# First FFN of a hybrid encoder trunk: second product by Strassen's algorithm, in a written order of three engines

## The chip, the core and the metric

The kernel runs on one core of one Trainium2 chip. The metric is device time in microseconds for one launch, from inputs in HBM to the output in HBM; the median of several runs is given. TensorE (PE) does the matrix products, VectorE (DVE) and ScalarE (ACT) the elementwise work, SyncE (SP) issues nearly all DMA transfers.

## The reference

One sequence of 512 tokens, model width 1024, two layers. Each layer is a token mixer (a short gated convolution in layer 0, a Mamba-2 SSD mixer in layer 1) followed by a SwiGLU FFN of width 2816. Each of these four sub-layers normalises, scales and shifts its input, and gates its normalised output by vectors that are computed from the conditioning vector c ("adaLN"):

```python
mod = (jax.nn.silu(c) @ ada_w + ada_b).reshape(bsz, DEPTH, 2, 3, D_MODEL)
...
shift, scale, gate = (mod[:, i, 1, k][:, None, :] for k in range(3))
h = rmsnorm(x, norm_g[i, 2]) * (1.0 + scale) + shift
gate, up = jnp.split(h @ w_in, 2, axis=-1)          # in swiglu_ffn
y = (jax.nn.silu(gate) * up) @ w_out                # 512x2816 @ 2816x1024
x = x + gate * rmsnorm(y, norm_g[i, 3])
```

All data are float32.

## The kernel before

Every float32 product is done in three matmuls: each operand is split into a rounded high part (a cast by ACT) and the low remainder (a subtraction by DVE), and high x high, high x low and low x high are summed in PSUM (`mm3`, `mm_tiles`, `product`). So each weight that arrives by DMA costs one ACT cast and one DVE subtraction (`split_w`) before TensorE can use it.

The first product of an FFN (`in_chunk`) makes one 128-feature block for all 512 tokens in 24 matmuls of 512 columns: 8 blocks of the inner dimension, three matmuls each. Features are taken in pairs, two gate blocks and two up blocks, so four chunks a pair and 11 pairs. In the first FFN (`ffn`), `ff_act` takes SiLU (ACT), multiplies by up (DVE) and splits the result for the second product.

The second product (`out_begin`) sums 22 feature blocks into four token tiles by two column halves, three matmuls each. Its end is interleaved with the next stage's beginning by `Boundary`: squares and roots for the norm, the residual `x`, the next norm `xn`, its transposes `tr`, scale and shift `u`, the split `hi`/`lo`, and the first matmuls `k` of the next stage for six feature blocks whose weights were made ahead (`lead`). The order of PE, ACT and DVE there is the written list `BOUNDARY`. Tokens 0 to 255 go first, tokens 256 to 511 after; `rest` finishes the second half's matmuls.

adaLN's product runs on DVE: `ada_madd` multiplies 512 columns of one 128-row block of `ada_w` by a column of c and adds it up; 8 of them are a set (2 MB of `ada_w`, loaded by `ada_load` in four transfers). `ada_keep` transposes and reduces the set, and `ada_fin` ends a unit of two sets with a small matmul and a few short DVE operations. There are 20 sets. In the first FFN `ada_next` does fourteen of them, interleaved with the feature pairs, and `put_gates` sends the gates through DRAM.

Outside blocks under `manual_schedule` a planner places the instructions: in the first FFN all engines, in the boundaries only those not named there. SP's order is the planner's everywhere but in the opening. Each engine and SP's queue run strictly in their order.

The last FFN (`last_ffn`) already does its second product by Strassen's algorithm. Activations are split into a 2 x 2 of blocks (two feature blocks of a pair, two token halves), weights into a 2 x 2 (two feature blocks, two column halves). `ff_pair` writes the activations and their sums, `build_sums` adds up the weight blocks and stores them in DRAM (`td`). Pass one multiplies three of the seven terms for all pairs, pass two the other four; `pa`, `pb`, `pz` are PSUM accumulators.

Of the kernel before, what the change touches and what calls it, by code (L numbers as in the profile page):

```python
# [35 lines left out]
def trunk_kernel(  # L36
# [52 lines left out]
    def turned(rws, cls, n):  # L89
        pt = aux_ps("ptr")  # L90
        pe.transpose(pt[:, :n], rws[:n, :], ident[:n, :n])
        dve.tensor_copy(cls, pt[:, :n])

    def other_vectors(stage):
# [9 lines left out]
        turned(stage[:, 0, :], mng, 16)  # L104
        turned(stage[:, 1, :], mcb, 32)
        turned(stage[:, 2, :], cols3, P)
        turned(d_rows.rearrange("p a b -> p (a b)"), dcol, 16)
# [182 lines left out]
    def w_at(w, hl, kk):  # L290
        return w[kk // 4][:, hl, kk % 4, :] if isinstance(w, list) else w[:, hl, kk, :]
# [90 lines left out]
    def out_begin(s, w, get_act, K, gg, xn_tile, first, lead, after):  # L382
# [47 lines left out]
        class Boundary:  # L430
# [21 lines left out]

            def sq(self, hf, t):
                st = self.st[t]
                if hf == 0:
                    st["s2"] = small(2)
                act.activation(self.junk(t, hf), ys[hf][t], AF.Square, accum_out=st["s2"][:, hf:hf + 1])

            def yg_(self, hf, t):
                self.yg[hf, t] = t2("yg")  # L460
                dve.tensor_mul(self.yg[hf, t], ys[hf][t], gg[0][:, self.cols(hf)])

            def b1(self, _, t):
                st = self.st[t]
                st["b1"] = small(1)
                dve.tensor_scalar(st["b1"], st["s2"][:, 0:1], 1.0 / D, EPS, MUL, ADD)

            def rt1(self, _, t):
                st = self.st[t]
                st["s1"] = small(1)  # L470
                act.activation(st["s1"], st["s2"][:, 1:2], AF.Sqrt, bias=st["b1"], scale=1.0 / D)
# [80 lines left out]
            def run(self, step):  # L552
                name, i = step.split("_")
# [3 lines left out]
                do(n, int(i))  # L557

# [47 lines left out]
    with ExitStack() as ph:  # L606
        ada_p.append(ph.enter_context(tc.tile_pool(name="adap", bufs=3, reuse_waits="tile")))
        actp = ph.enter_context(tc.tile_pool(name="actp", bufs=22, reuse_waits="tile"))
        gx = ph.enter_context(tc.tile_pool(name="gx", bufs=1, reuse_waits="tile"))
# [294 lines left out]
        def ffn_after(i):  # L904
            return lambda: load_w([(f_w_in[i], DFF + 256, 256)])

        begun = out_finish(out_begin(0, w_out0, lambda k: acts[k], KD, [gg], xn_tile, "aux",
                                     ffn_lead(0, tile4), ffn_after(0)))


        def ffn(s, i, begun, act_tile, gg_tile, xn_tile, ada, gates, lead, after):
            w1, w2 = f_w_in[i], f_w_out[i]
            acts = []
            h, lead_ps, rest, more = begun

            def ff_act(psg, psu, f):
                g = t2("g")
                act.activation(g, psg, AF.Silu)
                dve.tensor_mul(g, psu, g)
                a = act_tile(f"ff{f}")  # L920
                act.copy(a[:, 0, :], g)
                dve.tensor_tensor(a[:, 1, :], g, a[:, 0, :].bitcast(F32), SUB)
                acts.append(a)

            for f in range(0, NF, 2):
                if f == 0:
                    with tc.manual_schedule(engines={PE_ENGINE}):
                        for i in (0, 2, 1, 3, 4, 5):
                            rest(i)
                    pss = lead_ps[:4]  # L930
                elif f == 2:
                    pss = lead_ps[4:] + [in_chunk(w, h) for w in more]
                else:
                    pss = [in_chunk(w, h) for w in load_w([(w1, f * P, 256)]) + load_w([(w1, DFF + f * P, 256)])]
                for b in range(2):
                    ff_act(pss[b], pss[2 + b], f + b)
                ada(f)
                if f == 4:
                    list(vectors)
                if f == 18:  # L940
                    for q in gates:
                        put_gates(q)
                    gg = make_gg(s, gg_tile)
# [739 lines left out]
```

## Time and profile before

| | us |
|---|---|
| median of 3 runs (lowest, highest) | 1350.49 (1350.07, 1351.97) |
| the profiled execution | 1349.98 |
| its span, first to last instruction | 1348.1 |
| PE busy / DVE busy / ACT busy | 1337.3 / 912.0 / 561.7 |
| DMA moved, mean rate | 224.22 MB, 166 GB/s |

The stages of the first FFN, read off the order of matmuls in time: boundary from the convolution to about 222 us, first product to about 460, second product and boundary to the SSD layer from there to about 595. The last FFN runs from about 980 to the end.

In the rows quoted below, a group row gives line, engine, operation, output<-inputs, shape and count, then busy time in us and mean ns of one instruction, then the engine's idle time before them and what ended it. A row of waits gives who waited for whom: total us, times, longest us. A row of a stretch A:B gives for each engine its busy us and, in brackets, its instructions, then TensorE's granted clock, the mean busy share of the DMA engines, and GB/s. A timeline row begins with start and duration in us.

### The profile page before, as it was taken

What the parts mean: (1) busy time and instruction counts of PE and PEld (TensorE: products, weight loads), DVE (VectorE), ACT (ScalarE), POOL (GpSimd) and SP (SyncE); (2) the same over time, 40 slices, a digit from 0 to 9 for tenths busy, and PEclk for the clock granted to TensorE, in tenths of its full rate; (3) what the DMA queues carried; (4) which work ended last, traced back from release to release, by engine and by line L of the source; (5) the groups of instructions that cost most, each with busy time, mean ns of one, the idle gap of its engine ahead of it and who ended that gap; (6) DMA issues with size and microseconds to landing.
All of it is one profiled execution on the core that took longest, in us unless ns stands there. A gap on an engine that the chain in (4) does not pass through costs nothing.

```text
span 1348.1 us, 17657 instructions
## 1 busy us (share of the span) xinstructions
PE 1337.3 (99%) x6957; PEld 1124.6 (83%) x6957; DVE 912.0 (68%) x1512; ACT 561.7 (42%) x866; POOL 10.7 (1%) x27
## 2 busy tenths in 40 slices
PE   8999999999999999999999999999999999999997
PEld 7788889888888888898888888888899888888886
DVE  5799756787864222669888887787575555335884
ACT  5432346222222212655554445564473222223781
POOL 0000000000000000000000000000000000000000
PEclk9999999999999999999999999999999999999999
DMA  9978661577753222414543334423425987223752
GB/s 311 301 239 263 214 208 61 183 240 266 258 194 110 94 95 93 129 33 144 165 149 110 113 107 134 132 71 110 159 68 180 331 285 278 97 71 135 250 193 79
DMA packets 164759, 224.22 MB, mean 166 GB/s; under 512 B 7444, under 2 KB 112580, under 8 KB 162244
## 3 DMA queue, kind: packets, MB, share of 16 engines
q1 hardware_dynamic: 159776, 208.20, 47.3%
q10 hardware_dynamic: 4004, 12.77, 3.0%
q0 software_dynamic: 896, 2.11, 0.5%
q8 instruction: 55, 0.90, 0.3%
q14 instruction: 28, 0.23, 0.1%
HBM read 209.26 MB, written 13.80 MB: 165 GB/s over the span
## 4 chain that ended last, share of the span: by engine, by line
PE 97%; SPq 2%; DMA 1%; DVE 0%; issue 0%; ACT 0%; DVEq 0%; ACTq 0%
PE ip L294 19%; PE ip L295 18%; PE ip L296 18%; PE y L395 6%; PE y L397 6%; PE y L396 6%; PE li L294 3%; PE li L296 3%; PE li L295 3%; PE li L778 2%; PE yd L1185 1%; PE pb L1557 1%; PE pb L1559 1%; PE pb L1558 1%; SPq L641 1%; PE yo L1178 1%
## 5 line engine op out<-in xcount | busy, mean ns | idle before, releaser
L294 PE MATMUL ip<-h,whl 128*128 128x512 f32 x1096 | 431.2, 393 | 0.0
L296 PE MATMUL ip<-h,whl 128*128 128x512 f32 x1096 | 426.9, 389 | 0.0
L295 PE MATMUL ip<-h,whl 128*128 128x512 f32 x1096 | 426.6, 389 | 0.0
L294 PEld LDWEIGHTS ip<-h,whl 128*128 128x128 f32 x1096 | 205.8, 188 | 44.2 <-issue 2.4
L296 PEld LDWEIGHTS ip<-h,whl 128*128 128x128 f32 x1096 | 205.7, 188 | 43.4
L295 PEld LDWEIGHTS ip<-h,whl 128*128 128x128 f32 x1096 | 205.8, 188 | 41.5
L225 ACT CAST whl<-wst 128x1024 fp32r<-128x1024 f32 (+1 forms) x127 | 114.9, 926 | 190.2 <-PE ip L296 159.6
L226 DVE TENSOR_TENSOR whl<-wst,whl 128x1024 fp32r<-128x1024 f32 (+1 forms) x127 | 133.4, 1069 | 71.1 <-ACT whl L225 71.0
L146 DVE SCALAR_TENSOR_TENSOR ada_acc<-ada_st,csil,ada_acc 128x512 f32<-128x512 f32 x140 | 104.5, 748 | 24.2 <-DMA ada_st<-in_ada_w_dram 21.9
L226 DVE TENSOR_TENSOR whlo<-wsto,whlo 128x1024 fp32r<-128x1024 f32 x46 | 56.3, 1223 | 93.2 <-ACT whlo L225 93.1
L225 ACT CAST whlo<-wsto 128x1024 fp32r<-128x1024 f32 x46 | 48.3, 1051 | 111.1 <-PE y L397 83.6
L294 PE MATMUL li<-h,whl 128*128 128x256 f32 x288 | 83.3, 289 | 0.0
L296 PE MATMUL li<-h,whl 128*128 128x256 f32 x288 | 81.5, 283 | 0.0
L295 PE MATMUL li<-h,whl 128*128 128x256 f32 x288 | 81.5, 283 | 0.0
L395 PE MATMUL y<-whlo,ff 128*128 128x512 f32 x176 | 68.6, 390 | 0.0
L397 PE MATMUL y<-whlo,ff 128*128 128x512 f32 x176 | 68.5, 389 | 0.0
L396 PE MATMUL y<-whlo,ff 128*128 128x512 f32 x176 | 68.5, 389 | 0.0
L1052 DVE SCALAR_TENSOR_TENSOR cu<-ip,cols,cu 128x511 f32<-128x511 f32 (+2 forms) x84 | 62.7, 746 | 2.0
L244 DVE TENSOR_TENSOR whl<-wst,whl 128x1024 fp32r<-128x1024 f32 x46 | 55.0, 1218 | 8.0 <-ACT whl L243 7.9
L295 PEld LDWEIGHTS li<-h,whl 128*128 128x128 f32 x288 | 55.3, 192 | 0.0
L294 PEld LDWEIGHTS li<-h,whl 128*128 128x128 f32 x288 | 55.2, 192 | 0.0
L296 PEld LDWEIGHTS li<-h,whl 128*128 128x128 f32 x288 | 55.2, 192 | 0.0
(291 smaller groups left out, 1964.8 us busy)
## 6 DMA issues: line engine op xcount, KB each, us to landing
ada_st<-in_ada_w_dram SPq DMA_DIRECT2D x96, 512.0 KB, 5.6
wst<-in_f_w_in_dram SPq DMA_DIRECT2D x43, 1024.0 KB, 5.7
wst<-in_m_w_in_dram SPq DMA_DIRECT2D x14, 1024.0 KB, 5.3
tb<-in_f_w_out_dram SPq DMA_DIRECT2D x22, 512.0 KB, 7.2
td<-tb SPq DMA_DIRECT2D x11, 1024.0 KB, 7.7
wsto<-in_f_w_out_dram SPq DMA_DIRECT2D x10, 1024.0 KB, 4.9
wst<-in_m_w_in_dram SPq DMA_DIRECT2D x20, 512.0 KB, 4.1
wst<-in_a_w_in_dram SPq DMA_DIRECT2D x9, 1024.0 KB, 5.2
```

What stands on the lines that cost most here:

```text
L146: dve.scalar_tensor_tensor(acc, w, csil[:, k:k + 1], acc, MUL, ADD)
L225: act.copy(dst[:, 0, :nk, :], src)
L226: dve.tensor_tensor(dst[:, 1, :nk, :], src, dst[:, 0, :nk, :].bitcast(F32), SUB)
L244: lambda sw=sw, w=w: dve.tensor_tensor(w[:, 1, :nk, :], sw, w[:, 0, :nk, :].bitcast(F32), SUB)))
L294: pe.matmul(dst, w_at(w, 0, kk), a[:, 0, sl], start=start, stop=False)
L295: pe.matmul(dst, w_at(w, 0, kk), a[:, 1, sl], start=False, stop=False)
L296: pe.matmul(dst, w_at(w, 1, kk), a[:, 0, sl], start=False, stop=stop)
L395: pe.matmul(pst, a[:, 0, tk], wt[:, 0, kk, :], start=k == 0, stop=False)
L396: pe.matmul(pst, a[:, 0, tk], wt[:, 1, kk, :], start=False, stop=False)
L397: pe.matmul(pst, a[:, 1, tk], wt[:, 0, kk, :], start=False, stop=k == K - 1)
L778: pe.matmul(acc_of(i), w[:, part // 2, k, c0:c0 + P], h[kk][:, part % 2, :], start=(kk, part) == (0, 0), stop=(kk, part) == (KD - 1, 2))
L1052: dve.scalar_tensor_tensor(u[:, sft:], pst[:, :T - sft], w[3 - sft], u[:, sft:], MUL, ADD)
```

## The change

- The first FFN's second product becomes Strassen's, in two passes over eleven block pairs, like the last FFN's. The weight sums are made during the first product and go through DRAM (`td`, tensors te0 to te10).
- From the end of the previous boundary to the start of the SSD layer, PE, ACT and DVE run in the program's written order. `Queue` hands out adaLN steps (two multiply-adds each) and weight sums between the chunks: five steps and one set of sums per pair.
- The last four steps of the product are kept for a new boundary list, in which the four quadrants come out one after the other: `c12`, `d`, `c22`, `c21` are the recombinations on DVE, `ma`, `pb`, `p4` the products on PE.
- The weights for the SSD layer's first six chunks are made during the product (`load_ssd`, `make_ssd`).
- adaLN: one set moves to the convolution's boundary, eleven stay in the first FFN, two move to the last FFN, with the gate that they make. Four small vector transposes move to the convolution's boundary and use the other PSUM banks. The first layer's activation pool is closed before the FFN and the new pool takes its place in memory.

```diff
+    STRASSEN_BOUNDARY = """
+ma0 ma1 sq0_0 c12_0 yg0_0 sq1_0 b1_0 yg1_0 rt1_0 rc1_0 x0_0 x1_0 xs0_0 xs1_0 b3_0 rt3_0 pb_0 sq0_1
+c12_1 yg0_1 sq1_1 b1_1 yg1_1 rt1_1 rc3_0 rc1_1 xn0_0 xn1_0 p4_0 x0_1 x1_1 xs0_1 d_0 xs1_1 b3_1
+c22_0 rt3_1 pb_1 c21_0 sq1_2 rc3_1 yg0_2 sq0_2 xn1_1 xn0_1 b1_2 yg1_2 rt1_2 tr0_0 d_1 tr0_1 u0_0
+rc1_2 p4_1 c22_1 u0_1 x0_2 hi0_0 hi0_1 lo0_0 sq1_3 lo0_1 u0_2 xs0_2 u0_3 tr0_2 hi0_2 k0_0 c21_1
+hi0_3 lo0_2 sq0_3 lo0_3 b1_3 yg0_3 u0_4 tr0_3 u0_5 yg1_3 k0_1 hi0_4 x1_2 hi0_5 rt1_3 lo0_4 xs1_2
+lo0_5 k0_2 rc1_3 u0_6 x0_3 hi0_6 x1_3 xs0_3 k0_3 lo0_6 b3_2 xs1_3 rt3_2 b3_3 rc3_2 u0_7 rt3_3
+xn0_2 xn1_2 rc3_3 hi0_7 xn1_3 xn0_3 k0_4 lo0_7 tr1_0 tr1_1 u1_0 k0_5 u1_1 hi1_0 hi1_1 lo1_0 lo1_1
...
+        next(conv_parts[0])
+        list(vectors)
+        ada_next(1)
+        begun = out_finish(conv_parts)
+        ph0.close()
...
-                for b in range(2):
-                    ff_act(pss[b], pss[2 + b], f + b)
-                ada(f)
...
+        def first_ffn(begun, pool):
...
+            def sums_of(g):
...
+                dve.tensor_tensor(b11, b11, b12, ADD)
+                dve.tensor_tensor(b12, b12, b22, ADD)
+                dve.tensor_tensor(b22, b22, b11, ADD)
+                dve.tensor_tensor(b21, b21, b22, ADD)
+                dma(td[g], st)
+                yield
+            def ada_steps():
...
+                for n, (c0, kh) in enumerate(todo):
+                    if kh == 2 and n > 3 and c0 % D == 0:
+                        ada_fin(*ada_open.pop(0))
...
+                    for k in range(2):
+                        ada_madd(acc, st[n][:, k, :], kh * 2 + k)
+                    if n + 3 < len(todo):
+                        st.append(ada_load(*todo[n + 3]))
+                    if kh == 3:
+                        ada_keep(c0, acc)
+                    yield
...
+                def add(self):
+                    next(self.sums.pop(0))
+                    self.load_sums()
...
+            with tc.manual_schedule(engines={PE_ENGINE, mybir.EngineType.Activation, mybir.EngineType.DVE}):
...
+                for g in range(2, NG2):
...
+                    pss = [in_chunk(now[0], h)]
...
+                        load_pair(2 * g + 2)
+                    gs = [silu(pss[0])]
+                    split(0)
+                    jobs.step()
+                    pss.append(in_chunk(now[1], h))
...
+                    gs.append(silu(pss[1]))
+                    split(1)
+                    jobs.add()
+                    jobs.step()
+                    pss.append(in_chunk(now[2], h))
...
+                    up0(pss[2], gs[0])
+                    split(2)
+                    jobs.step(2)
...
+                    pss.append(in_chunk(now[3], h))
...
+                    up1(pss[3], gs[1])
+                    split(3)
+                    jobs.step()
...
+                for i in range(N2 - TAIL):
+                    a6, a22, w8, w4 = ready[i][:4]
+                    if i < NG2:
+                        product(pa, a6[:, :, 0, :], w4, i == 0)
+                        product(pb, a6[:, :, 2, :], w8[1], i == 0)
+                        product(pz, a6[:, :, 1, :], w8[0], i == 0)
+                    else:
+                        product(p4, a22, ready[i][4], i == NG2)
+                        product(pa, a6[:, :, 0, :], w8[0])
+                        product(pb, a6[:, :, 1, :], w4)
+                        product(pz, a6[:, :, 2, :], w8[1])
...
+                    if i + 4 < N2:
+                        load_out(i + 4)
+                    if i + 3 < N2 - 1:
+                        make_act(i + 3)
+                        make_w(i + 3)
...
+                    own[f"c12_{t}"] = lambda t=t: dve.tensor_tensor(nr1[t], nr1[t], pz[t], ADD)
+                    own[f"d_{t}"] = lambda t=t: dve.tensor_tensor(np1[t], pb[t], np1[t], SUB)
+                    own[f"c22_{t}"] = lambda t=t: dve.tensor_tensor(c22[t], c22[t], np1[t], SUB)
+                    own[f"c21_{t}"] = lambda t=t: dve.tensor_tensor(np1[t], np1[t], p4[t], ADD)
...
+            if f in (6, 12):
+                c0 = ada_sets.pop(0)
+                acc = pool.tile([P, T], F32, tag="keep", name="ada_acc", bufs=6)
+                for k in range(KD):
+                    st = pool.tile([P, T], F32, tag="keep", name="ada_st", bufs=6)
+                    dma(st, ada_w[k * P:(k + 1) * P, c0:c0 + 512])
+                    ada_madd(acc, st, k)
+                ada_keep(c0, acc)
+            if f == 16:
+                ada_fin(*ada_open.pop())
+                put_gates(3)
```

`load_out` fetches a step's weights into the buffers in which they are split, `make_act` and `make_w` split its activations and weights, `early` (`ma`) does the first two products of the last four steps for one token tile.

More of the change, by code (lines that the diff above doesn't have):

```diff
@@ L103, in other_vectors @@
         yield
[L104 to L107, printed above, removed]
+        turned(stage[:, 0, :], mng, 16, mm_ps)
+        turned(stage[:, 1, :], mcb, 32, mm_ps)
+        turned(stage[:, 2, :], cols3, P, mm_ps)
+        turned(d_rows.rearrange("p a b -> p (a b)"), dcol, 16, mm_ps)
     mods = consts.tile([P, 96], F32, name="mods")
@@ L380, in trunk_kernel, with out_begin @@
     LATE = 3
-    def out_begin(s, w, get_act, K, gg, xn_tile, first, lead, after):
+    STRASSEN_BOUNDARY = """
[6 more added lines that the diff above has]
+xn0_2 xn1_2 rc3_3 hi0_7 xn1_3 xn0_3 k0_4 lo0_7 tr1_0 tr1_1 u1_0 k0_5 u1_1 hi1_0 hi1_1 lo1_0 lo1_1
+tr1_2 u1_2 k0_6 u1_3 hi1_2 hi1_3 lo1_2 lo1_3 u1_4 u1_5 tr1_3 hi1_4 k0_7 hi1_5 lo1_4 lo1_5 u1_6
+u1_7 hi1_6 k1_0 hi1_7 lo1_6 lo1_7 k1_1
+""".split()
+    def out_begin(s, w, get_act, K, gg, xn_tile, first, lead, after, own=None):
         ys = [None, None]
@@ L451, in m1b, with begins @@
                 mm_tiles(1, self.tail[1][2:], [t])
+            def begins(self, t):
+                return 1 if own and t > 1 else 0
             def sq(self, hf, t):
                 st = self.st[t]
-                if hf == 0:
+                if hf == self.begins(t):
                     st["s2"] = small(2)
@@ L552, in run @@
             def run(self, step):
+                if own and step in own:
+                    return own[step]()
                 name, i = step.split("_")
@@ L557, in run @@
                 do(n, int(i))
+        if own:
+            ys = own["ys"]
+            bd = Boundary(None)
+            bd.ws = own["ws"]
+            for step in STRASSEN_BOUNDARY:
+                bd.run(step)
+            return bd.h, [bd.acc[i] for i in range(6)], bd.rest, after()
         def finish():
@@ L905, in ffn_after @@
             return lambda: load_w([(f_w_in[i], DFF + 256, 256)])
[L907 to L913, printed above, removed]
-            h, lead_ps, rest, more = begun
-            def ff_act(psg, psu, f):
-                g = t2("g")
[L918 to L932, printed above, removed]
-                else:
-                    pss = [in_chunk(w, h) for w in load_w([(w1, f * P, 256)]) + load_w([(w1, DFF + f * P, 256)])]
-                for b in range(2):
-                    ff_act(pss[b], pss[2 + b], f + b)
-                ada(f)
[L938 to L943, printed above, removed]
-            return out_finish(out_begin(s, w2, lambda k: acts[k], NF, [gg], xn_tile, "aux", lead, after))
@@ L954, in trunk_kernel @@
+        begun = first_ffn(begun, ph.enter_context(tc.tile_pool(name="mf", bufs=1, reuse_waits="tile")))
         h, lead_ps, rest, wz1 = begun
-        assert not ada_sets and not ada_open
+        assert len(ada_sets) == 2 and not ada_open
     with ExitStack() as ph:
```

299 lines of the change are left out of this document (284 added, 15 removed).

## The prediction

> **What bounds the kernel now.** I read the page's busy shares first, then whom TensorE waited for, then its cadence in the product that the change rewrites.
>
> ```profile
> span 1348.1 us, 17657 instructions
> PE 1337.3 (99%) x6957; PEld 1124.6 (83%) x6957; DVE 912.0 (68%) x1512; ACT 561.7 (42%) x866; POOL 10.7 (1%) x27
> PE ptr L91 <- DMA rows<-in_c_dram: 2.3, 1, 2.3
> PE xtr L690 <- DVE xn L672: 0.4, 1, 0.4
> PE ada_pe L207 <- DMA ada_st<-in_ada_w_dram: 0.4, 2, 0.2
> PE y L395 <- ACT r L1217: 0.2, 1, 0.2
> PE xtr L690 <- ACT xn L670: 0.2, 1, 0.2
> ```
>
> The last five rows are all the waits that TensorE has: 3.5 us together, by their lines in the opening and in the SSD layer, none in the first FFN. A busy PE row need not mean a full pipe, so the cadence has to be seen too: first and last row of a run of 46 matmuls in the first FFN's second product, then one of that product's three lines as a group (the other two have the same count).
>
> ```profile
> 489.80 0.39 PE L396 MATMUL y<-whlo,ff 128*128 128x512 f32 x1
> ...
> 500.00 0.39 PE L396 MATMUL y<-whlo,ff 128*128 128x512 f32 x1
> L395 PE MATMUL y<-whlo,ff 128*128 128x512 f32 x176 | 68.6, 390 | 0.0
> ```
>
> 45 steps in 10.20 us: a 512-column matmul starts every 0.2267 us, though each row lasts 0.39 (they overlap). So time in this stretch is the number of matmuls times 0.2267, and the other engines only matter where they make TensorE wait. A chunk of the first product (24 matmuls) takes 5.44 us, a pair of feature blocks (four chunks) 21.76.
>
> **What the change removes.** Today's second product has 3 x 176 = 528 matmuls. In the new one, eleven block pairs take 3 products of 6 matmuls in the first pass and 4 in the second: 11 x 18 + 11 x 24 = 462, with the same operand shapes. The last FFN already runs that form:
>
> ```profile
> L1557 PE MATMUL pb<-w,a 128*128 128x512 f32 x66 | 25.7, 389 | 0.0
> L1557 PE MATMUL pa<-w,a 128*128 128x512 f32 x44 | 17.1, 389 | 0.0
> L1557 PE MATMUL pz<-w,a 128*128 128x512 f32 x44 | 17.1, 389 | 0.0
> 1250.00:1280.00 30.00, 30.00 (x134) 24.86 (x133) 25.71 (x36) 21.37 (x32) 0.00 (x0) 1.00 0.75 250
> ```
>
> Three lines of 66 + 44 + 44 are 462, with no idle before them, and 30 us of that stage hold 134 records (30 / 0.2267 = 132): the same cadence. So 66 fewer matmuls x 0.2267 = **-14.96 us**. Transposes and the adaLN matmuls only move.
> [...]
>
> **Whether DVE keeps up in the first product.** The orders of PE, ACT and DVE are now written out, so a late DVE operation holds up all that stands behind it. Prices:
>
> ```profile
> L226 DVE TENSOR_TENSOR whl<-wst,whl 128x1024 fp32r<-128x1024 f32 x91 | 110.5, 1220 | 57.9 <-ACT whl L225 57.8
> L225 ACT CAST whl<-wst 128x1024 fp32r<-128x1024 f32 x91 | 94.8, 1048 | 171.7 <-PE ip L296 159.6 <-issue 7.9 <-PE ada_ps L136 4.2
> L1426 ACT ACTIVATE g<-ip 128x512 f32<-128x512 f32 x18 | 10.8, 599 | 75.6 <-PE ip L296 75.6
> L146 DVE SCALAR_TENSOR_TENSOR ada_acc<-ada_st,csil,ada_acc 128x512 f32<-128x512 f32 x140 | 104.5, 748 | 24.2 <-DMA ada_st<-in_ada_w_dram 21.9
> L144 DVE TENSOR_SCALAR ada_acc<-ada_st,csil 128x512 f32<-128x512 f32 x20 | 9.5, 476 | 3.2 <-DMA ada_st<-in_ada_w_dram 3.1
> L131 DVE STREAM_TRANSPOSE tr<-ada_acc 128x512 f32<-128x512 f32 x20 | 13.8, 699 | 0.0
> L1452 DVE TENSOR_TENSOR tb<-tb 128x512 f32<-128x512 f32 x11 | 7.6, 692 | 0.3
> L1428 DVE TENSOR_TENSOR za<-ip,g x10: 414/424/425, 1035.1 to 1230.9; 128x256 f32<-128x256 f32 x10
> 363.00:385.00 22.00, 22.00 (x98) 18.17 (x98) 19.45 (x30) 6.40 (x9) 0.00 (x0) 1.00 0.83 274
> ```
>
> DVE per pair: four weight corrections, 4.88; five adaLN steps of two multiply-adds, which is 1.25 sets of 0.48 + 7 x 0.75 + 0.70 for the transpose and about as much for the reduction = 7.1, so 8.9; four weight sums of 0.69, 2.76; gating and activation sums, one of 0.69 and six of 0.42, 3.2. Together **19.7 us of 21.76**, 91%. The present kernel's busiest pair holds 19.45 of 22 (last row) and TensorE doesn't stop in it. ACT has four casts and two SiLUs, 5.4 us. The rate itself costs nothing: what hides it is 2.1 us of margin a pair, and the weights' lead. In the written order the first correction runs from 5.44 + 0.60 + 1.05 = 7.1 to 8.3 us of a pair and is wanted at 21.76: 13 us of lead.
> The end of an adaLN unit has less. It is a small matmul that stands in TensorE's own order, three steps after the DVE reduction that it reads. Laying the prices along a pair, step 1 ends at 9.8 us; after the second chunk the correction ends at 13.8, the sums at 16.6, step 2 at 18.1; then gating and a correction to 20.1, steps 3 and 4 to 23.1, gating and a correction to 26.7, step 5 to 28.2. A reduction takes 1.4 more. Counting pairs from 0, the unit closed after the first chunk of pair 4 reads one that ends at 24.5 of the pair before, 2.7 of its own, and comes up at 5.44; the one closed after the last chunk of pair 8 reads one that ends at 19.5 and comes up at 21.76. So a DVE lag of 2.5 us there stops TensorE; the three others have 5 us or more. And DVE does wait for adaLN's transfers:
>
> ```profile
> DVE ada_acc L146 <- DMA ada_st<-in_ada_w_dram: 14.3, 9, 2.9
> 1045.00:1079.00 34.00, 34.00 (x151) 28.15 (x151) 20.66 (x29) 8.69 (x11) 0.00 (x0) 1.00 0.96 333
> ada_st<-in_ada_w_dram SPq DMA_DIRECT2D x96, 512.0 KB, 5.6
> td<-tb SPq DMA_DIRECT2D x11, 1024.0 KB, 7.7
> ```
>
> The first row covers 255 to 385 us, six pairs: 2.4 us a pair. A new pair moves 2 MB of weights, 1 MB into the sums, 1 MB back and 2.5 MB of adaLN: 6.5 x 1.049 MB in 21.76 us, 313 GB/s, where the heaviest stretch of the trace reached 333 with the engines 96% busy. So the waits stay or grow, and they eat the margin. Bounds: 0 (the lag never exceeds that cover) and 6 us (3 us too much at each of the two places); nearer to the first, since waits of today's size just fill the margin: **+1.0**.
>
> **The second product.** A first-pass step is 18 x 0.2267 = 4.08 us of TensorE, a second-pass step 5.44.
>
> ```profile
> L1481 DVE TENSOR_TENSOR a<-zb,a 128x768 fp32r<-128x768 f32 x11 | 10.5, 955 | 5.0 <-ACT a L1480 5.0
> L1481 DVE TENSOR_TENSOR w<-r,w 128x512 fp32r<-128x512 f32 x23 | 15.6, 684 | 0.7 <-ACT w L1480 0.7
> r<-td SPq DMA_DIRECT2D x10, 512.0 KB, 5.6
> ```
>
> With 1.22 for the widest form, DVE needs 0.96 + 0.68 + 1.22 = 2.9 us for a first-pass step and 0.96 + 3 x 0.68 + 1.22 = 4.2 for a second-pass one; ACT's casts of the same data are no longer. A transfer leaves as a step ends and is wanted three steps, 12.2 us, later: 5.6 to land, 1.05 and 1.22 to split make 7.9. Around the change of pass the second-pass operands are made during 4.08 us steps, beside weights for the next stage and the negated partial sums, some 3 us too much, against 12 us made ahead. Cost 0; without that lead, these 3 us.
>
> **The boundary to the SSD layer.** Today it has no gap, and this to spare:
>
> ```profile
> 579.66 1.34 ACT L508 ACTIVATE xn<-x,ss 128x512 f32<-128x512 f32 x2
> 580.50 0.88 DVE L510 TENSOR_SCALAR xn<-x,ss 128x512 f32<-128x512 f32 x2
> 583.06 0.60 PE L517 MATMUL xtr<-ident,xn 128*128 128x128 f32 x4
> L478 DVE SCALAR_TENSOR_TENSOR x<-yg,ss,x 128x512 f32<-128x512 f32 x24 | 17.2, 748 | 0.4
> 560.98 0.16 DVE L474 RECIPROCAL ss<-ss 128x1 f32<-128x1 f32 x1 [0.74 <-ACT ss L471]
> ```
>
> The normalised rows end at 581.4, their transposes start at 583.1: 1.7 us. The new order adds two recombinations of 0.69 on DVE behind the last products of the second token half, which leaves 0.3. In the first half, DVE passes six operations of 0.69, two of 0.75, one of 0.44 and five of 0.16 before tile 1 is normalised (6.9 us), and ACT adds two of 0.67: 8.3, with the hand-offs up to 8.8, under 36 matmuls (8.16). Bounds 0 and 3 us (both halves late by a few operations); by these sums the misses are small: **+1.0**.
>
> **What moves.** One adaLN set (2 MB, 7.1 us of DVE) goes to the conv boundary, two go to the last FFN:
>
> ```profile
> 165.00:203.00 38.00, 38.00 (x171) 31.50 (x170) 22.73 (x40) 18.00 (x40) 0.00 (x0) 1.00 0.62 208
> 1146.00:1180.00 34.00, 34.00 (x152) 28.15 (x151) 12.38 (x19) 7.77 (x9) 0.00 (x0) 1.00 0.28 95
> ```
>
> DVE has 15 us free in the first stretch and 21 in the second: cost 0, and up to 2 us if a lead weight or a matmul came late behind them.
>
> **The sum.** The profiled run took 1349.98 us around its span of 1348.1; the median is 0.51 above it. 1349.98 - 14.96 + 1.0 + 1.0 = 1337.0, at the median **1337.5**.
>
> **Rivals.**
> *DVE lags in the first product.* For it: 91% load, and the waits above. Against it: the last pair has no adaLN work, so a lag ends there. 3 to 10 us lost: about **1342**.
> *The transfers set the pace, and it is slower.* SP issues in its order, and in the last FFN it stands before a load until an earlier store has landed:
>
> ```profile
> SPq L1443 <- DMA td<-tb: 31.0, 8, 8.3
> ```
>
> If adaLN loads queue behind that, each step waits. With 1.5 us at each of five a pair takes 19.7 + 7.5 = 27.2, 5.4 over; eight pairs lose 43.5, less 13 of lead, so 30: 1335.5 + 30 = **1366**. The point where it is slower than before is a wait w with 8 x (w - 2.1) - 13 = 17.7, 5.9 us a pair. Against it: 2.4 a pair today, the longest single one 2.9. For it: 313 of 333 GB/s.
> [...]
> *The boundary misses by more.* Both halves late, 3 to 5 us: about **1341**.
> *The change does not do what it says.* Stalls of 12.3 to 17.7 us give the 14.96 back: about **1350**.
>
> **Chances.** Forecast 0.55, with its own range from 1335.5 (no stall) to 1340; DVE lag 0.20; boundary 0.07; nothing left 0.05; slower 0.13. Reaching over the two middle rivals to 1345.5, and 0.3 below the case without stalls, leaves about 0.2 out. Faster 0.82, within 0.2% (2.7 us, about what this measurement can tell from no change) 0.05, slower 0.13.
>
> **What would show it.** Right: 462 matmuls in that product at 0.2267, waits of PE under 3 us in all of the first FFN, less than 1 us idle before each set of transposes in the boundary. Wrong: PE waiting for the adaLN matmul's operand or for weights in pairs 4 to 9 (DVE lag); DVE waiting over 5 us a pair for adaLN's transfers while SP stands before the sums' next load (transfers); gaps before the transposes (boundary).

## The result, and the profile after

The changed kernel takes **1335.79 us** (median of 4 runs, 1335.1 to 1336.71) where the kernel before took 1350.28 in the same comparison (1350.03 to 1351.97): a ratio of 0.989, with a 95% interval of 0.9873 to 0.9908. The profiled run took 1335.2 us, 14.8 less than the profiled run before. 1337.5 was predicted, between 1335.2 and 1345.5: the median lies 0.6 us above the lower end, the shortest run just below it.

From the kernel after: its span, its busy engines, and from the timeline a short wait of TensorE (start, duration, engine, line, operation; in brackets the idle time before it and who ended it).

```profile
span 1333.4 us, 17900 instructions
PE 1322.1 (99%) x6891; PEld 1111.7 (83%) x6891; DVE 997.5 (75%) x1671; ACT 588.8 (44%) x918; POOL 10.7 (1%) x27
975.37 0.55 PE L535 MATMUL xtr<-ident,xn 128*128 128x128 f32 x3 [0.28 <-ACT xn L526]
```

TensorE has 66 matmuls fewer and is busy 15.2 us less. VectorE (DVE) has 85 us more to do. None of TensorE's waits (4.4 us, five kinds) lies in the first FFN: 3.9 us are in the opening, 0.2 in the SSD layer, and the one shown, at 975 us, in the boundary before the last FFN. Next the groups of the second product, for one of its three lines (L1118 and L1119 have the same counts).

```profile
L1117 PE MATMUL pb<-w,a 128*128 128x512 f32 x44 | 17.1, 389 | 0.0
L1117 PE MATMUL p<-w,a 128*128 128x512 f32 x22 | 8.6, 393 | 0.0
L1117 PE MATMUL pz<-w8h,a 128*128 128x512 f32 x22 | 8.6, 390 | 0.0
L1117 PE MATMUL pa<-w,a 128*128 128x512 f32 x22 | 8.6, 389 | 0.0
L1117 PE MATMUL pz<-w,a 128*128 128x512 f32 x22 | 8.6, 389 | 0.0
L1117 PE MATMUL pa<-w8h,a 128*128 128x512 f32 x22 | 8.6, 389 | 0.0
```

44 + 5 x 22 = 154 a line, 462 in all, with no idle time before any. Milestones from the views by line: the first matmuls of the SSD layer (`tokT`), of the last FFN's second product (`pa`) and of the first FFN's (`y`) in the kernel before. The columns are durations in ns (least, median, longest), then the first and last start in us.

```profile
L994 PE MATMUL tokT<-ident,raw x4: 221/222/243, 600.0 to 600.2; 32*128 32x32 f32 x4
L1557 PE MATMUL pa<-w,a x44: 389/389/389, 1236.1 to 1323.8; 128*128 128x512 f32 x44
L395 PE MATMUL y<-whlo,ff x176: 389/389/477, 450.8 to 570.3; 128*128 128x512 f32 x176
```

The same in the kernel after, and the first of its second product in the first FFN (last row):

```profile
L1361 PE MATMUL tokT<-ident,raw x4: 221/222/243, 584.9 to 585.1; 32*128 32x32 f32 x4
L1937 PE MATMUL pa<-w,a x44: 389/389/389, 1221.9 to 1309.6; 128*128 128x512 f32 x44
L1117 PE MATMUL pa<-w,a x22: 389/389/389, 450.6 to 492.1; 128*128 128x512 f32 x22
```

The SSD layer starts 15.1 us earlier, so the whole gain is made by then. The first FFN's second product starts nearly when that of the kernel before did (450.6 and 450.8, the last row of each; not at about 460, as the list of stages ahead of the prediction has it), and from there to the SSD layer it takes 134.3 us instead of 149.2: 14.9 less. By the start of the last FFN's second product 0.9 us are given back (14.2 earlier): 0.5 of them in the SSD layer, since the last FFN's first matmuls (`li`) start at 1014.4 for 1029.0, with the wait of 0.3 us shown above among them, and 0.4 in the stage that now holds two adaLN sets and their closing matmul. The span ends 14.7 earlier.

**The first product** is where the kernel might have lost time. Two stretches of 22 us (busy time of PE, its weight loads, DVE, ACT, POOL, with counts; granted clock; share of the DMA engines; GB/s):

```profile
266.00:288.00 22.00, 22.00 (x99) 18.21 (x99) 19.12 (x32) 5.18 (x6) 0.00 (x0) 1.00 0.98 341
353.00:375.00 22.00, 22.00 (x100) 18.24 (x99) 21.03 (x31) 5.42 (x7) 0.00 (x0) 1.00 0.92 323
```

The waits of DVE, ACT and SP's queue there (us in total, times, longest), and from the timeline the longest of the eight waits of DVE for a cast, with that cast, and a typical one, with the SiLU before its cast:

```profile
DVE whl L244 <- ACT whl L243: 18.3, 8, 6.0
DVE ada_acc L146 <- DMA ada_st<-in_ada_w_dram: 1.2, 2, 0.9
ACT whl L243 <- DMA wst<-in_f_w_in_dram: 14.9, 3, 6.7
SPq L979 <- DMA te<-tb: 22.1, 7, 5.3
419.20 1.05 ACT L243 CAST whl<-wst 128x1024 fp32r<-128x1024 f32 x1 [6.41 <-DMA wst<-in_f_w_in_dram]
420.29 1.22 DVE L244 TENSOR_TENSOR whl<-wst,whl 128x1024 fp32r<-128x1024 f32 x1 [5.98 <-ACT whl L243]
...
286.00 0.60 ACT L955 ACTIVATE g<-ip 128x512 f32<-128x512 f32 x1 [3.90 <-PE ip L297]
287.57 1.23 DVE L244 TENSOR_TENSOR whl<-wst,whl 128x1024 fp32r<-128x1024 f32 x1 [2.29 <-ACT whl L243]
```

And how long an adaLN tile takes to land there (KB each, median us from issue to landing):

```profile
ada_st<-in_ada_w_dram SPq DMA_DIRECT2D x39, 512.0 KB, 7.2
```

DVE works up to 96% of a stretch and the DMA engines up to 98%, at 341 GB/s, and TensorE (22.00 of 22.00) never stops. DVE's waits for adaLN's tiles were 14.3 us in 9 before and are 1.2 in 2 now, though such a tile takes longer to land (7.2 us here, 5.5 in the six pairs of those 14.3 us). They also come at a slower pace: five a pair here, 37 in those six pairs.

Some lateness shows at the weights instead. Three casts start late on ACT because the weights have not landed (14.9 us), and one of them holds up DVE, by 6.0 us. The seven other waits of DVE for a cast, 12.3 us, are not lateness: there ACT had waited for TensorE's chunk (as at 286.00) and not for weights, so DVE was ahead of its work. SyncE does stand before the sums' next load until the store of earlier sums has landed (22.1 us in 7).

**The boundary**, by the timeline (start, duration, engine, line, operation): the first and the last of 35 matmuls, the transposes behind them, and the normalisation of tile 1 on ACT that the transposes read.

```profile
544.70 0.39 PE L1118 MATMUL pb<-w,a 128*128 128x512 f32 x1
...
551.46 0.71 ACT L526 ACTIVATE xn<-x,ss 128x512 f32<-128x512 f32 x1
...
552.40 0.39 PE L1119 MATMUL pb<-w,a 128*128 128x512 f32 x1
552.64 1.03 PE L535 MATMUL xtr<-ident,xn 128*128 128x128 f32 x8
```

34 steps in 7.70 us are 0.2265 each, and the transposes follow 0.24 after the last product. The normalised tile is ready at 552.17, 0.47 us ahead of the transposes, and no wait is booked here.

### The profile page after: what moved, and what is told of

Same layout as the page of the kernel before. It is cut to its first block, busy times and chain, and to the rows that moved or that the text cites. A ratio compares the mean times of both kernels' runs of the same rounds, so it can differ in the third digit from the quotient of the medians.

```text
span 1333.4 us, 17900 instructions
## 1 busy us (share of the span) xinstructions
PE 1322.1 (99%) x6891; PEld 1111.7 (83%) x6891; DVE 997.5 (75%) x1671; ACT 588.8 (44%) x918; POOL 10.7 (1%) x27
## 4 chain that ended last, share of the span: by engine, by line
PE 95%; SPq 2%; DMA 1%; ACT 1%; DVE 1%; issue 0%; DVEq 0%; ACTq 0%
PE ip L295 19%; PE ip L297 19%; PE ip L296 19%; PE y L408 3%; PE y L410 3%; PE y L409 3%; PE li L295 3%; PE li L297 3%; PE li L296 3%; PE li L807 2%; PE yd L1552 1%; PE pb L1937 1%; PE pb L1939 1%; PE pb L1938 1%; SPq L670 1%; PE yo L1545 1%
## 5 line engine op out<-in xcount | busy, mean ns | idle before, releaser
L225 ACT CAST whl<-wst 128x1024 fp32r<-128x1024 f32 (+1 forms) x79 | 70.5, 918 | 118.5 <-PE ip L297 109.1
L243 ACT CAST whl<-wst 128x1024 fp32r<-128x1024 f32 x82 | 83.7, 1045 | 80.5 <-PE ip L297 57.2
L244 DVE TENSOR_TENSOR whl<-wst,whl 128x1024 fp32r<-128x1024 f32 x82 | 98.9, 1219 | 26.7 <-ACT whl L243 26.2
L226 DVE TENSOR_TENSOR whl<-wst,whl 128x1024 fp32r<-128x1024 f32 (+1 forms) x79 | 81.9, 1058 | 42.3 <-ACT whl L225 42.2
L408 PE MATMUL y<-whlo,ys 128*128 128x512 f32 x128 | 50.7, 396 | 0.2 <-ACT r L1584 0.2
L410 PE MATMUL y<-whlo,ys 128*128 128x512 f32 x128 | 49.9, 390 | 0.0
L409 PE MATMUL y<-whlo,ys 128*128 128x512 f32 x128 | 49.8, 389 | 0.0
L1793 ACT ACTIVATE g<-ip 128x512 f32<-128x512 f32 x18 | 10.8, 600 | 74.9 <-PE ip L297 74.9
```

The costliest lines, as they stand in the source:

```text
L225: act.copy(dst[:, 0, :nk, :], src)
L226: dve.tensor_tensor(dst[:, 1, :nk, :], src, dst[:, 0, :nk, :].bitcast(F32), SUB)
L243: later.append((lambda sw=sw, w=w: act.copy(w[:, 0, :nk, :], sw), lambda sw=sw, w=w: dve.tensor_tensor(w[:, 1, :nk, :], sw, w[:, 0, :nk, : ...
L244: lambda sw=sw, w=w: dve.tensor_tensor(w[:, 1, :nk, :], sw, w[:, 0, :nk, :].bitcast(F32), SUB)))
L408: pe.matmul(pst, a[:, 0, tk], wt[:, 0, kk, :], start=k == 0, stop=False)
L409: pe.matmul(pst, a[:, 0, tk], wt[:, 1, kk, :], start=False, stop=False)
```

## The experiments

Most of these are single runs. The kernel before took between 1350.3 and 1353.6 us beside them (medians), and between 1349.95 and 1355.88 in thirteen runs beside the first, so single runs are read by the starts of their stages: pass one, the first `pa` of L1117, at 450.6, and the SSD layer at 584.9 in the kernel after.

### Is it the 66 matmuls?

66 matmuls were put back into pass one, into two accumulators that are overwritten later.

```diff
-                p4 = []
+                p4 = [mm_ps("p4") for _ in range(2)]
...
                         product(pz, a6[:, :, 1, :], w8[0], i == 0)
+                        product(p4, a6[:, :, 1, :], w8[1], i == 0)
```

> The changed kernel with 66 matmuls put back: in each of the eleven first-pass steps six more of the same shape go to the two PSUM banks that the fourth product uses later; their sums are overwritten, nothing else differs. If time in the first FFN is the number of matmuls times 0.2267 us, a first-pass step goes from 4.08 to 5.44 us and the whole returns by 14.96 us, to 1350.7 us. If the first pass were already held by DVE or by transfers (DVE is 84 to 98% busy there), the added matmuls would fill gaps and the time would come out at 1345 or less.

Measured: 1349.95 us (1349.42 to 1350.49), ratio to the kernel before 0.999 (0.9981 to 1.0). The SSD layer starts 15.0 us later:

```profile
L1362 PE MATMUL tokT<-ident,raw x4: 221/222/243, 599.9 to 600.1; 32*128 32x32 f32 x4
```

15.0 / 66 = 0.227 us each, and no new wait in this FFN. The count of matmuls is the whole gain.

### Two adaLN sets back in the first product

All thirteen sets that are left run in the first product, six steps a pair instead of five, none in the last FFN.

```diff
-                todo = [(c0, kh) for c0 in ada_sets[:-2] for kh in range(4)]
-                del ada_sets[:-2]
+                todo = [(c0, kh) for c0 in ada_sets for kh in range(4)]
+                del ada_sets[:]
...
-                    jobs.step()
+                    jobs.step(2)
...
-            if f in (6, 12):
-                c0 = ada_sets.pop(0)
...
```

> The spreading of adaLN undone in part: the two sets of the last FFN go back to the first product (six steps a pair in place of five), and nothing of them is left in the last FFN. DVE's durations per pair become 19.7 + 1.8 = 21.5 of 21.76 us, the transfers 7 MB or 337 GB/s, where the stretches of the changed kernel move 315 to 341 with the DMA engines 91 to 98% busy. If the margin is as small as worked out, TensorE stops in pairs 4 to 9 and the first FFN grows by 3 to 15 us. If three steps of prefetch and the weights' lead still cover it, the time stays within 1 us of 1335.8 and the spreading bought nothing.

Measured: 1349.61 us. The waits of TensorE and of ACT in the first product:

```profile
PE ada_ps L136 <- DVE row L132: 8.3, 3, 4.3
ACT whl L243 <- DMA wst<-in_f_w_in_dram: 47.9, 10, 7.9
```

The start of pass one, by line:

```profile
L1117 PE MATMUL pa<-w,a x22: 389/389/389, 462.4 to 503.9; 128*128 128x512 f32 x22
```

Two stretches of 6 us around the longest stop:

```profile
384.00:390.00 6.00, 4.33 (x11) 3.56 (x12) 5.79 (x10) 1.04 (x1) 0.00 (x0) 0.53 1.02 360
390.00:396.00 6.00, 6.00 (x25) 4.85 (x25) 5.86 (x12) 1.06 (x1) 0.00 (x0) 0.90 0.87 296
```

One step a pair more, 1.8 us of DVE and 0.5 MB, costs 11.8 us in the first product and another 2.4 at the change of pass, nearly the whole gain. TensorE stops where the prediction said it would, at the matmuls that close a unit. The stops are 8.3 us. Around the longest one (4.35 us, to 385.67) the granted clock is half: 0.50 in each of the six stretches of 1 us from 385 to 391, 0.71 and 0.88 in those beside them. So a stretch of 6 us with a mean of c holds 2 x (1 - c) x 6 us of half clock, here 5.6 + 1.2 = 6.8 us. By the stretches of 1 us they lie from 384.4 to 391.2, so 1.3 us fall into the stop itself, and in the other 5.5 us, where a matmul starts every 0.43 us (386.69 to 389.67), about 2.8 us of work are lost (an estimate, half of them).

This leaves open what makes DVE late: its own rate (19.7 + 1.8 = 21.5 of 21.76 us a pair), the transfers (7 MB a pair, 337 GB/s), or only the place of the closing matmul. Two more runs, both with the thirteen sets, separate them.

*The closing four steps later in TensorE's order* (the last unit's three later):

```diff
-                    if kh == 2 and n > 3 and c0 % D == 0:
+                    if kh == 2 and n > 7 and c0 % D != 0:
...
-                for _ in range(3):
+                for _ in range(6):
```

> The kernel after with all thirteen adaLN sets in the first product (six steps a pair, none in the last FFN), as in the earlier run of that, and with each unit's closing matmul four steps later in TensorE's order (the last unit's three steps later). If the place of the closing matmul is what bound that run: the waits on the closing matmul (8.3 us in three there) fall below 1 us, the granted clock stays 1.00, pass one starts within 2 us of 450.7 (462.4 there) and the time is 1336 to 1339 us. If DVE's rate itself bound it (by the sums 19.7 + 1.8 = 21.5 us of 21.76 a pair, more with waits for transfers): TensorE waits elsewhere, for corrected weights, and pass one starts at 457 or later, the time is 1343 to 1350 us.

Measured: 1355.11 us, pass one at 461.6. The waits of TensorE and of ACT:

```profile
PE pb L1117 <- DVE row L138: 4.7, 1, 4.7
PE ip L295 <- ACT whl L243: 4.1, 1, 4.1
PE ip L297 <- DVE whl L244: 2.1, 1, 2.1
ACT whl L243 <- DMA wst<-in_f_w_in_dram: 80.3, 10, 19.0
```

The first product loses 11.0 us where it lost 11.8: no wait on a closing matmul is left in it, and TensorE stops a little later for weights instead, which landed late (ACT waited 80 us for them, 48 with the closings in their old place). The 4.7 us in the first row come with the edit: the last closing now stands right before pass one, and `pb` needs the accumulator that DVE has yet to read. So the place of the closings wasn't the cause.

*The sums stored for the first pair only.* The second product reads that one pair's sums eleven times; every DVE operation stays.

```diff
-                dma(td[g], st)
+                if g == 0:
+                    dma(td[0], st)
...
-                    dma(w8[:, 1].bitcast(F32), td[g][:, 1:3, :])
+                    dma(w8[:, 1].bitcast(F32), td[0][:, 1:3, :])
...
-                    dma(w48[:, 1].bitcast(F32), td[g][:, 0:4:3, :])
+                    dma(w48[:, 1].bitcast(F32), td[0][:, 0:4:3, :])
```

> The kernel after with all thirteen adaLN sets in the first product (six steps a pair, closing matmuls where the kernel after has them), and with the sums of the weights stored for the first pair only; the second product then loads that one pair's sums eleven times, so its result is not the reference's. That takes away 1 MB of 7 a pair (289 GB/s instead of 337) and SP's standing for the stores, and leaves every DVE operation in its place. If transfers made the run with thirteen sets slow: the waits on the closing matmul (8.3 us there) and for casts of late weights fall under 1 us, pass one starts at 450.5 to 452 (462.4 there) and the time is 1336 to 1338 us. If DVE's rate (21.5 us of 21.76 a pair) made it slow: pass one starts at 458 or later and the time is 1345 to 1350 us.

Measured: 1340.15 us, on a chip where the kernel before took 1353.62. The one stop at a closing matmul, by the timeline (idle time before it in brackets):

```profile
292.85 0.41 PE L136 MATMUL ada_ps<-row,blocks 128*128 128x32 f32 x2 [1.63 <-DVE row L132]
```

The stretch behind it, and a later one:

```profile
294.00:300.00 6.00, 6.00 (x21) 4.76 (x20) 5.86 (x10) 0.00 (x0) 0.00 (x0) 0.72 0.94 283
...
359.00:381.00 22.00, 22.00 (x98) 18.22 (x98) 21.27 (x36) 5.19 (x6) 0.00 (x0) 1.00 0.87 286
```

The start of pass one, by line (line numbers of the second product are one higher here):

```profile
L1118 PE MATMUL pa<-w,a x22: 389/389/389, 454.1 to 495.6; 128*128 128x512 f32 x22
```

With 1 MB a pair less, 8.3 of the 11.8 us are gone. What is left, 3.5 us, is one stop of 1.63 us and 3.4 us of half clock behind it (2 x 0.28 x 6; 0.50 in the stretches of 1 us from 295 to 297), which cost about 1.7 (an estimate, half of them). It follows a wait of DVE for one adaLN tile early in the first pairs (5.5 us, to 268.7). From 300 us on, DVE is busy up to 97% of a stretch with six steps a pair, and TensorE never waits. So **the transfers** made the run with thirteen sets slow (the bytes of the stores, or the queue's standing for them; this run takes both away), and DVE's rate alone does not bind even there. Neither 452 (transfers alone) nor 458 (rate alone) was right to the microsecond; 454.1 stands nearer to the first.

### One more megabyte a pair

The kernel after with each pair's sums stored twice, the second time to a place that nobody reads.

```diff
                 dma(td[g], st)
+                dma(td2[g], st)
```

`td2` is a second list of such tensors in DRAM.

> The kernel after with the weights' sums stored twice, the second time to a place that nobody reads: 1 MB more a pair, 7.5 x 1.049 MB in 21.76 us, 361 GB/s where the busiest stretch of the kernel after reached 341 with the DMA engines 98% busy. If transfers are next to bind in the first product: DVE's waits for adaLN's tiles come back (over 10 us together, 1.2 now), some of them reach TensorE, and the time is 1338 to 1350 us. If there is room in them still: over 350 GB/s in a stretch, waits under 5 us, and the time within 1 us of 1335.8.

Measured: **1373.62 us**, 23 slower than the kernel before. Waits of TensorE and of DVE:

```profile
PE ada_ps L136 <- DVE row L132: 25.7, 4, 7.9
DVE whl L244 <- ACT whl L243: 53.3, 9, 13.6
DVE ada_acc L146 <- DMA ada_st<-in_ada_w_dram: 2.6, 3, 1.1
```

The start of pass one, by line:

```profile
L1119 PE MATMUL pa<-w,a x22: 389/389/389, 488.9 to 530.3; 128*128 128x512 f32 x22
```

This is more than was expected, 38.3 us in the first product. Again the waits are not at adaLN's tiles (2.6 us) but at casts (53.3 us, 47.0 of them at casts that waited for late weights), and TensorE meets them where DVE's lag comes up first, at the closing matmuls. The stops are 28.0 us with three small ones for weights; for the remaining 10 the granted clock falls to between 0.77 and 0.84 in the four stretches of 22 us that hold the long stops.

The bytes alone hardly explain this. At 341 GB/s 7.5 MB take 23.1 us, 1.3 more than a pair has: over eight pairs 10 us, less than the prediction's 13 of lead (an estimate). In fact only 3% more was moved per second than in the kernel after (from 250 to 440 us 321 GB/s, and 312 there). And SyncE stood before the sums' loads until the added store had landed:

```profile
SPq L980 <- DMA tf<-tb: 30.8, 9, 6.0
```

So the standing of the queue is the likelier part; no run adds bytes without it.

### More work on DVE

Three and then eight products of two tiles were added for every pair, 0.69 us each, which are written again to the same place.

```diff
                     up1(pss[3], gs[1])
+                    for _ in range(0 if last else 3):
+                        dve.tensor_mul(zb[-1][:, 0:4:3, :], pss[3].rearrange("p (a f) -> p a f", a=2),
+                                       gs[1].rearrange("p (a f) -> p a f", a=2))
```

> Three more DVE operations per pair in pairs 2 to 9 of the first product: the 512-wide gating product of the fourth chunk is done over again with the same result, 0.69 us each, 2.07 a pair. By summed durations (19.7 us) that fills the 2.1 us of margin: 0 to +1 us, lag growing to a few us. By start-to-start distances (the rows overlap by about 0.07 us, which makes some 18 us a pair) 1.6 us of margin remain and nothing changes.

> The same with eight more, 5.5 us a pair. By summed durations a pair takes 25.2 us on DVE, 3.5 over TensorE's 21.76, 28 over eight pairs, less the 13 us of lead: +15 us, about 1350. By start-to-start distances 23.6 us, 1.9 over, 15 in all, less 13: +2 us, about 1338. If the closing matmuls of the adaLN units bind first, TensorE waits before them with some 2.5 us of cover only: +10 us or more even by the second count.

Measured with three: 1339.40 us, pass one 4.3 us later. One stop, at the last closing matmul, by the timeline:

```profile
447.50 0.41 PE L136 MATMUL ada_ps<-row,blocks 128*128 128x32 f32 x2 [2.52 <-DVE row L132]
```

The stretch that holds it:

```profile
447.00:453.00 6.00, 5.50 (x18) 4.41 (x19) 5.90 (x9) 2.30 (x3) 0.00 (x0) 0.72 0.48 173
```

2.52 us, and 0.28 x 12 = 3.4 us at half clock (0.50 in the stretches of 1 us from 448 to 451), which cost about 1.7 (an estimate, half of them). With eight: 1366.59 us, pass one 30.6 later. TensorE's waits:

```profile
PE ada_ps L136 <- DVE row L132: 15.8, 3, 6.8
PE ip L297 <- DVE whl L244: 4.4, 1, 4.4
```

20.2 us of stops, and the other 10 with a lower granted clock around them (0.52 to 0.91 in seven stretches of 6 us): twice the 15 us that the sum of durations gave. The margin of 2.1 us a pair was about right: 3 x 0.69 just use it up, 8 x 0.69 exceed it by 3.4 a pair.

Both again with the closing matmuls later, by the same edit as above:

> The kernel after with three more DVE operations a pair, as in the earlier run of that, and with the closing matmuls four steps later (the last three steps later). If their place bound it: no wait on a closing matmul, the granted clock stays 1.00 from 447 to 455 us, pass one starts within 0.7 us of 450.7 (454.9 there), the time is 1335.1 to 1336.7 us. If DVE's rate bound it: 1339 us again, with the wait at another place.

> The kernel after with eight more DVE operations a pair, as in the earlier run of that, and with the closing matmuls later. Here both theories have DVE over its rate: 19.7 + 8 x 0.69 = 25.2 us of 21.76, some 3.5 us a pair over nine pairs, 31, less the 13 us by which weights are ahead and the 9 that the last pair has without adaLN steps: about 10 us late at the end. By the place of the closing matmul the time falls from 1366.6 to about 1345 to 1352, with waits for corrected weights only and less half clock; by the rate alone it stays within 5 us of 1366.

Measured with three: pass one starts at 450.9, so the stop is gone from the first product, but the time is 1342.97 us. TensorE now waits 4.7 us at `pb` (as in the run with thirteen sets), and the granted clock is 0.92 in the 22 us that hold this wait (447 to 469). The last closing stands right before pass one there, and what ends the wait is DVE's reading of its accumulator (`row`, L138). How much of those 4.7 us is DVE's lag and how much the edit, no run without the three operations shows. With eight: 1365.23 us, pass one at 474.4, and the stops move from the closings to the weights (8.6 us in 5) and to the added operations themselves (`zb`, 6.3 in 2).

That is what the rate alone led one to expect. In both, a later place moved the stops and did not remove them; with eight it saved 7 us of the first product (474.4 instead of 481.2) and 1.4 in all.

### The adaLN tiles fetched two steps ahead, not three

```diff
-                st = [ada_load(*todo[n]) for n in range(3)]
+                st = [ada_load(*todo[n]) for n in range(2)]
...
-                    if n + 3 < len(todo):
-                        st.append(ada_load(*todo[n + 3]))
+                    if n + 2 < len(todo):
+                        st.append(ada_load(*todo[n + 2]))
```

> adaLN's transfers are asked for two steps ahead in place of three; the work is the same. In the changed kernel DVE waits 1.2 us in all for them although they take 7.2 us to land. If three steps of prefetch are what covers that, two steps (8.7 us on average, 4 to 6 between close steps) do not: DVE waits 10 us or more over the first product, and TensorE loses 0 to 4 us. If the waits went because fewer sets are left in this stage, they stay under 3 us and the time within 1 us of 1335.8.

Measured: 1335.88 us, DVE's waits for adaLN 0.7 us in all, pass one at 450.7. The depth of the prefetch is not what made those waits small. (With thirteen sets they are 6.6 us in 3.)

### ACT and DVE left to the planner in the first product

Only TensorE's order stays written there; from the second product on all three are.

```diff
-            with tc.manual_schedule(engines={PE_ENGINE, mybir.EngineType.Activation, mybir.EngineType.DVE}):
+            with tc.manual_schedule(engines={PE_ENGINE}):
                 ws, splits = [], []
...
+            with tc.manual_schedule(engines={PE_ENGINE, mybir.EngineType.Activation, mybir.EngineType.DVE}):
                 pa = [aux_ps("pa") for _ in range(2)]
```

> The written order undone for ACT and DVE in the first product only: there the planner places them (PE's order stays written); second product and boundary are unchanged. If the work fits whatever the order (19.7 of 21.76 us), the time is within 1 us of 1335.8, and DVE's waits for adaLN transfers show what the order does to them: about 2.4 us a pair as in the kernel before if the order's spacing removed them, about 0.1 if the smaller number of sets did. If the written order is what keeps TensorE fed, PE waits appear and the time is 1341 or more.

Measured: 1336.79 us (1336.65 to 1338.04), ratio to the kernel before 0.9899 (0.9882 to 0.9915), which overlaps the interval of the kernel after. The first product has the same length, 207.0 to 452.8 = 245.8 us against 204.8 to 450.6. The 2.2 us by which it starts later in the profiled run are lost in the conv layer's end, 1.6 of them in one wait of `y` for DVE. The written order of ACT and DVE is worth nothing in the first product by itself. What the order does change is where DVE waits for transfers:

```profile
DVE tb L983 <- DMA tb<-in_f_w_out_dram: 24.4, 8, 5.2
DVE ada_acc L146 <- DMA ada_st<-in_ada_w_dram: 3.6, 5, 1.2
```

For adaLN's tiles that is 3.6 us, about 0.4 a pair, neither the 2.4 nor the 0.1 that were expected; but DVE waits 24.4 us for the weights to be summed (`tb`), for which it doesn't wait at all in the written order. TensorE stops at neither.

### The boundary, one product later

The `pb` products of tile 1 (`pb_1`, twelve matmuls) were moved behind the first transposes, which takes 2.72 us of cover from the chain that normalises tile 1.

```diff
-c22_0 rt3_1 pb_1 c21_0 sq1_2 rc3_1 yg0_2 sq0_2 xn1_1 xn0_1 b1_2 yg1_2 rt1_2 tr0_0 d_1 tr0_1 u0_0
+c22_0 rt3_1 c21_0 sq1_2 rc3_1 yg0_2 sq0_2 xn1_1 xn0_1 b1_2 yg1_2 rt1_2 tr0_0 pb_1 d_1 tr0_1 u0_0
```

> In the boundary's list the step pb_1 (twelve matmuls, 2.72 us) moves from before the first transposes tr0_0 to behind them. If tile 1's chain is as long as its cover (8.3 to 8.8 us under 8.16, 0.3 us waited), taking 2.72 us of cover away makes TensorE wait 2 to 3 us before tr0_0 and the time goes to about 1338.3. If the chain only looked that long because DVE stands behind the products themselves (the recombination of p4_0 is in front of tile 1's last reciprocal), the wait stays under 0.8 us.

Measured: 1338.37 us; from the start of pass one to the SSD layer 137.7 us instead of 134.3. TensorE's wait for the transposes' input:

```profile
PE xtr L535 <- ACT xn L526: 2.0, 1, 2.0
```

The transposes wait 2.0 us where they did not wait before. (The expectation's 0.3 us is the wait at 975 us, in another boundary.) The chain had 0.5 us to spare and lost 2.72 of cover, so it is nearly as long as its cover. Another 0.6 us is a wait at the change of pass, which the edit doesn't touch; 0.8 of the 3.4 us are not accounted for by waits.

## Why the prediction was right

**The removed matmuls, -14.96: right.** 462 are there, at 0.2265 us, and the stage from the second product to the SSD layer is 14.9 us shorter. The run with 66 more gives the price back at 0.227 each. The trace's cadence was the right one.

**DVE in the first product, +1.0: it was 0.** The prices were a little high: from 266 to 420 us DVE is busy 19.0 of 22 us, 18.8 a pair, where 19.7 were summed. The 2.1 us of margin were about right: three more operations (2.07 us) bring one stop of 2.52 us, eight more cost 30.6. The places were right in kind, since TensorE stops at closing matmuls in five of these kernels. Three statements failed. "So the waits stay or grow": DVE's waits for late transfers are 1.2 us for adaLN and 6.0 for a weight, 0.9 a pair over eight pairs where 2.4 were carried over. The closings with the least cover were said to be those of pairs 4 and 8: they have 4.4 and 2.2 us (2.7 and 2.3 were worked out), but the last one, in the last pair, has 0.5, and it is the one that stops with three more operations. And "the last pair has no adaLN work" is wrong, which is why: it holds a whole set. Its multiply-adds by line, then the end of its reduction and the closing matmul from the timeline of the kernel after:

```profile
L146 DVE SCALAR_TENSOR_TENSOR ada_acc<-ada_st,csil,ada_acc x7: 744/751/753, 428.8 to 442.2; 128x512 f32<-128x512 f32 x7
443.68 0.69 DVE L132 TENSOR_REDUCE row<-tr 128x16 f32<-128x512 f32 x1
444.87 0.30 PE L136 MATMUL ada_ps<-row,blocks 128*128 128x32 f32 x2
```

So the allowance was not needed, but by half a microsecond, at a place that the prediction had taken for safe.

**The transfers as the rival: not what happened, but the nearest danger.** Parts of its mechanism are in the kernel (SP stood 22.1 us before loads of sums), but the 7.2 us of DVE's waits behind late transfers are well inside the margin. The prediction's condition for slower than before was 5.9 us of waits a pair. The run with 1 MB more has 47.0 + 2.6 us, 6.2 a pair, and is slower; the prediction's sum, 8 x (6.2 - 2.1) - 13 = 20 us, stands beside 28.0 us of stops measured there, and with the granted clock of 0.77 to 0.84 around them pass one starts 38 later. The chance of 0.13 rested on 313 of 333 GB/s; the kernel moved 312 over 190 us and reached 341.

**The second product, 0: right** in the profiled run, which has no wait in it. Kernels with other edits show 0.2 to 2.4 us at the change of pass (`pa` behind `np`, the negated partial sums; 2.4 with thirteen sets), two of them, with the prefetch and the boundary edited, 0.6 though they change nothing there. So there is little to spare at this place. Whether the 1.5 us between the two shorter and the two longer runs of the kernel after come from there was not tried.

**The boundary, +1.0: it was 0.** The chain was summed at 8.3 to 8.8 us under 8.16; it ended 0.5 us ahead of its transposes, so it was 0.6 to 1.1 us shorter than that. The run with one product less of cover shows that there is little more to spare. The allowance for a second miss, in the second token half, was not needed either.

**What moves, 0: it was about 0.4** in the last FFN's first product, inside the bound of 2. The four transposes that went to the conv layer's end cost there what they cost before: the first product starts 0.9 us later (204.8 for 203.9) and takes 1.1 less.

**The sum.** -14.9 in the second product and boundary, 0.2 less ahead of it, 0.5 more in the SSD layer, 0.4 more in the last FFN's first product and 0.5 less behind the start of its second make the -14.7 of span; between the medians it is -14.5. The small terms are those of one profiled run each, and waits explain only 0.3 of them. The time is 1.7 us under the forecast because neither of the two allowances of 1.0 came true: it is the prediction's sum without stalls, 1335.5, to 0.3 us. It lies inside the range by the count and the cadence; that the allowances cost nothing was left open, not foreseen.

## What to carry to other kernels

Where TensorE never waits, count its matmuls and multiply by the cadence of the trace (0.2267 us here): this gave the gain to 0.2 us where the changed stage ends. What decides whether the gain is kept is the margin of the engines beside it, and that is best asked with one more step, one more operation or one more megabyte: here three small operations a pair cost 4 us of the first product, one more adaLN step 12, and a second store of the sums 38. Where transfers are late, look for them at every consumer, since the order decides which one meets them: at the weights in the written order (ACT waited 14.9 us for them), at the weights to be summed with the planner's (DVE, 24.4 us). And look at what ended each wait before it is called lateness: of DVE's 18.3 us behind casts, 12.3 were an engine ahead of its work.

## What the runs showed of the hardware

In these runs a stop of TensorE could cost more than its length: the one of 2.52 us (three more operations) put pass one 4.3 us later. After it, and after the one of 1.63 us (thirteen sets, sums not stored), the granted clock was half, 0.50, for 3.4 us; around the one of 4.35 us (thirteen sets), for 6.8. After two others in the run with thirteen sets, of 2.00 us and this one of 1.92, it was 1.00 in every stretch of 1 us:

```profile
293.25 0.41 PE L136 MATMUL ada_ps<-row,blocks 128*128 128x32 f32 x2 [1.92 <-DVE row L132]
```

A third there, of 2.4 us at the change of pass, cost little more than itself: from the start of pass one to the SSD layer 137.1 us, where the kernel after takes 134.3. So in these runs length alone does not decide it, nor does the half clock begin with the stop's end: by stretches of 1 us it begins 1.6 us after the end of the stop of 1.63, 0.4 after that of 2.52, and 1.3 before the end of the one of 4.35. What does decide it was not tried.

In the kernel after the DMA engines ran at 98% of a 22 us stretch and 341 GB/s with no harm to TensorE (busy 22.00 us of it, clock 1.00). With 8% more bytes asked for (thirteen sets, 7 MB a pair for 6.5) TensorE lost 12 us in the first product, of which 8.3 go when the sums are not stored; with 15% more (7.5 MB, and one more store to stand for) it lost 38. How much of this is bytes and how much the queue's standing was not separated.
